# Hybrid encoder trunk: band added on VectorE, rotary product from PSUM, first convolution steps on ScalarE, more weight buffers

## The chip, the cores and the metric

The kernel runs on one core of a Trainium2 chip, as one program. The metric is the time of one execution in device microseconds. In the profile the engines are PE (TensorE, matrix products), PEld (its weight loads), DVE (VectorE), ACT (ScalarE), POOL (GpSimd) and SP (SyncE, whose queue issues most DMAs).

## The reference, cut to what matters

The reference is a two-layer bidirectional encoder on two inputs with shared weights: a prompt of 1024 tokens and a sample of 512, both 1024 wide, in float32.

```python
def even_layer(...):                       # layer 0
    u = h @ w_in
    glu, a_gate, q, k, v, b_gate = split_cols(u, EVEN_SPLITS)
    a = a_val * jax.nn.sigmoid(a_glu)
    a = layernorm(depthwise_conv(a, conv_w, conv_b), ln_g, ln_b)      # 31 taps
    a = jax.nn.silu(a) * jax.nn.silu(a_gate)
    q = apply_rope(q, cos, sin); k = apply_rope(k, cos, sin)
    o = windowed_gqa(q, k, v, sink) * jax.nn.silu(b_gate)             # keys within 128 tokens
    return jnp.concatenate([a, o], axis=-1) @ w_out

def windowed_gqa(q, k, v, sink):
    scores = jnp.where(mask, q . k * dh ** -0.5, -jnp.inf)
    probs = softmax(concatenate([scores, sink_logit]))[..., :-1]
    return probs . v

def odd_layer(...):                        # layer 1
    # differential attention: softmax(q1.k1) - lam * softmax(q2.k2), per-head norm, gate
    # Mamba-2 scans forward and backward, behind a 5-tap depthwise convolution
    return jnp.concatenate([c, d], axis=-1) @ w_out
```

Rotary embedding is `x * cos + rotate_half(x) * sin`. An RMS norm stands ahead of each layer and at the end, and each layer adds its input.

## The kernel before

**Tiles.** Activations lie with channels on the 128 partitions and tokens along the free dimension, in three chunks `g` of 512 tokens (two of the prompt, one of the sample). A projection (`proj`, L273 to L283) makes a 128x512 block: over eight slices of the input it adds three float32r products, L280 (high weight by high input), L281 (high by low) and L282 (low by high), so 24 matmuls into one PSUM bank.

**Weights.** `load_w` (L258) brings a tile of weights in two halves of 128x512. For each half SP issues the load into `wr` (L267), ACT writes the rounded high part `wh` (L268) and POOL subtracts it to make the low part `wl` (L269). Each of the three has three buffers for the whole kernel, so one and a half tiles. A half serves all three chunks.

**Stages.** `phase` opens pools for each stage from the table `PHASES`: A1 (gated convolution, rotary q and k, v), A2 (sliding attention, output projection of layer 0), B1a (short convolution), B1z (z and v of layer 1), B1b (scans, rotary of layer 1), B2 (differential attention), O1 (the last output projections). `SHARED` lists tiles with buffers for all stages, among them `e2`, the 128x512 scratch of the evacuations (four). Projections have one PSUM bank `pj` and, in some stages, further `pjx`: four in A1, one in A2, none in B1b.

**Order.** The code puts units of work beside one another (`merge`, `spread`). A planner then orders the instructions of each engine with a timeline of its own, by when operands and buffers come free there, and the order is fixed in the program. On the chip each engine takes its instructions in that order and waits on semaphores. So another buffer count or another instruction can change the order of much else.

**Convolution (A1).** For each of four blocks of channels `glu_units` makes the gated input `a`, and `conv_units` (L435) filters it on DVE: odd taps, even taps and their sums accumulate in three tiles `fir`. `begin` starts them with L444, L446 and L447 (multiply by the first tap, two of them with a bias), then `taps` runs L453, L456 and L458, each of which reads two tiles of SBUF. `conv_ln` (L475) normalizes all four.

**Rotary.** `rope` (L375) is called 15 times in A1 and 24 times in B1b. ACT copies the product from PSUM to `r` (L378), four DMAs exchange the half heads into `rs` (L381), DVE multiplies `r` by the cosine in place (L382), POOL multiplies `rs` by the sine (L383), DVE adds (L384) and SP stores (L385). `r` and `rs` are `e2` tiles.

**Sliding attention (A2).** For each block `b` of 128 queries and each key head `g`, `scores` handles four query heads:

```python
T_.matmul(o, qh, kk, start=True, stop=False)                 # L553
T_.matmul(o, ql, kk, start=False, stop=False)                # L554
T_.matmul(o, ident_r, cr[...], start=False, stop=True)       # L555, adds 0 or -1e30
V.tensor_reduce(out=mx, in_=o, op=ALU.max, negate=True)      # L558
V.tensor_tensor(out=mx, in0=mx, in1=nsink, op=ALU.min)       # L559
S.activation(out=pr, in_=o, func=AF.Exp, bias=mx, accum_out=den)   # L561
```

There are 12 blocks, so 96 such tiles: 64 of 384 keys and 32 of 256. The scores have three PSUM banks, `s1`. The probabilities `pr` (eleven tiles) are scaled on POOL (L569), transposed on PE (L584), split into high and low parts (L201 on ACT, L202 on DVE, to `pT`) and multiplied by the values (L587, L588); L589 and L590 put out the result. `values` runs one group behind `scores`. Gate projections (`gate2`: ACT L371, DVE L372) and the output projection run beside it.

**Others that the change touches.** `xbc` (L705) is the short convolution: L713 starts it on DVE, L716 runs the other four taps, L718 applies the activation. `diff_units` in B2 has, for each block of queries, L979 (square of a denominator times a constant), L981, L982 (the ratio) and L984 (difference of the two maps).

## Time and profile before

| quantity | value |
|---|---|
| median of 3 runs | 1711.17 us (1710.85 to 1715.9) |
| profiled execution, its own time | 1710.5 us |
| its span, first to last instruction | 1708.7 us |
| mean granted TensorE clock | 0.979 |
| instructions | 22696 |
| HBM traffic over the span | 127 GB/s |

The profiled execution is one of its own, 0.7 us below the median; about 1.8 us of its time lie outside the span. A line of the waits names who waited, for what, the sum in us, how often and the longest. A line of a group gives source line, engine, operation, tiles and shapes, the count, then busy time, mean duration in ns, and the idle time of the engine ahead of it with what ended it. `pjx<-x,wl` means that a tile `pjx` is written from `x` and `wl`. A matmul's duration runs from its start to its modelled end, and matmuls overlap.

### The profile page before, as it was taken

Reading aid. Unit: us, or ns where it says so; the run is one execution under the profiler, and the core shown is the slowest. Engines: PE = TensorE matmul, PEld = TensorE weight load, DVE = VectorE, ACT = ScalarE, POOL = GpSimd, SP = SyncE. Lnnn points to the kernel's source line nnn. Section 1 sums busy time; section 2 is a strip of 40 time slices with the busy share of each in tenths; the row PEclk is TensorE's granted clock in tenths of the full one; section 3 lists DMA queues with packets and bytes.
Section 4 is the critical chain, followed back from the end, with each engine's and each line's share of the span. In section 5 each row is a group of like instructions: output and inputs, shape, how many; then the busy total and the mean of one; then the engine's idle time right before and its main releaser. Section 6 shows DMA issues by size and latency. Waiting matters only on the chain.

```text
span 1708.7 us, 22696 instructions
## 1 busy us (share of the span) xinstructions
PE 1586.7 (93%) x7868; PEld 1303.6 (76%) x7868; DVE 1132.5 (66%) x1631; ACT 708.1 (41%) x1440; POOL 677.5 (40%) x531
## 2 busy tenths in 40 slices
PE   4998998889988989999999999989998999999997
PEld 3776787668777867867788887778877877888887
DVE  6788999954788786646664003796635677678554
ACT  6210111144676664433433112222225767668542
POOL 4244333333656545631311004654444534442340
PEclk9999999989999999999999999999999999999999
DMA  9011023335455447731433216664553545442562
GB/s 371 29 53 47 32 74 98 113 104 175 126 169 184 150 145 232 236 111 37 131 105 130 78 50 189 198 180 141 158 150 124 149 131 147 138 133 75 178 198 99
DMA packets 159109, 229.45 MB, mean 134 GB/s; under 512 B 18279, under 2 KB 70567, under 8 KB 158994
## 3 DMA queue, kind: packets, MB, share of 16 engines
q1 hardware_dynamic: 157074, 227.40, 42.2%
q8 instruction: 62, 1.02, 0.3%
q0 software_dynamic: 1920, 0.59, 0.2%
q14 instruction: 53, 0.43, 0.1%
HBM read 153.15 MB, written 64.55 MB: 127 GB/s over the span
## 4 chain that ended last, share of the span: by engine, by line
PE 30%; DMA 7%; DVE 4%; issue 4%; POOL 2%; SPq 2%; ACT 2%; POOLq 0%; DVEq 0%; ACTq 0%
PE ms L992 3%; PE pj L280 3%; PE pj L281 3%; PE pj L282 3%; DMA e<-e 2%; PE pjx L747 2%; PE pjx L746 2%; PE pjx L748 2%; PE s L967 2%; PE s L968 2%; PE pjx L280 1%; PE pjx L281 1%; PE pjx L282 1%; POOL e L383 1%; PE tr L390 1%
## 5 line engine op out<-in xcount | busy, mean ns | idle before, releaser
L269 POOL TENSOR_TENSOR wl<-wr,wh 128x512 fp32r<-128x512 f32 (+1 forms) x169 | 274.0, 1625 | 366.0 <-ACT wh L268 325.7
L282 PE MATMUL pjx<-x,wl 128*128 128x512 f32 (+1 forms) x712 | 286.4, 404 | 19.9 <-POOL wl L269 19.9
L280 PE MATMUL pjx<-x,wh 128*128 128x512 f32 (+1 forms) x712 | 287.4, 404 | 12.5 <-DVE e L372 8.0
L281 PE MATMUL pjx<-x,wh 128*128 128x512 f32 (+1 forms) x712 | 287.9, 405 | 6.3 <-DVE x L202 5.0
L280 PE MATMUL pj<-x,wh 128*128 128x512 f32 x604 | 247.4, 410 | 9.3 <-DVE e L372 5.0
L281 PE MATMUL pj<-x,wh 128*128 128x512 f32 x604 | 244.3, 404 | 3.9 <-DVE x L202 3.9
L282 PE MATMUL pj<-x,wl 128*128 128x512 f32 x604 | 241.9, 400 | 0.0
L268 ACT ACTIVATE wh<-wr 128x512 fp32r<-128x512 f32 (+1 forms) x169 | 105.5, 625 | 205.9 <-PE pjx L281 86.5
L282 PEld LDWEIGHTS pjx<-x,wl 128*128 128x128 f32 (+1 forms) x712 | 135.2, 190 | 55.5 <-POOL wl L269 23.0
L280 PEld LDWEIGHTS pjx<-x,wh 128*128 128x128 f32 (+1 forms) x712 | 134.8, 189 | 49.6 <-DVE e L372 10.4
L281 PEld LDWEIGHTS pjx<-x,wh 128*128 128x128 f32 (+1 forms) x712 | 134.8, 189 | 41.4 <-DVE x L202 6.6
L280 PEld LDWEIGHTS pj<-x,wh 128*128 128x128 f32 x604 | 115.6, 191 | 36.0 <-DVE e L372 6.1
L281 PEld LDWEIGHTS pj<-x,wh 128*128 128x128 f32 x604 | 115.3, 191 | 30.2 <-DVE x L202 5.1
L282 PEld LDWEIGHTS pj<-x,wl 128*128 128x128 f32 x604 | 115.3, 191 | 26.5 <-issue 0.2
L383 POOL TENSOR_TENSOR e<-e,cs 128x512 f32<-128x512 f32 x39 | 64.8, 1660 | 106.5 <-DMA e<-e 96.9
L976 ACT ACTIVATE pr<-s,nmx 128x1024 f32<-128x1024 f32 (+1 forms) x96 | 93.3, 975 | 27.6 <-DVE nmx L970 15.7
L177 POOL TENSOR_TENSOR r<-v,mhalf 128x4 f32<-128x4 f32 (+2 forms) x37 | 33.0, 892 | 140.5 <-DVE v L173 91.6
L992 PE MATMUL ms<-v,pT 128*128 128x128 f32 x640 | 81.2, 278 | 6.5 <-ACT pT L989 4.0
L992 PEld LDWEIGHTS ms<-v,pT 128*128 128x128 f32 x640 | 77.9, 193 | 10.6 <-ACT pT L989 4.4
L970 DVE TENSOR_REDUCE nmx<-s 128x1 f32<-128x1024 f32 x64 | 76.8, 1217 | 10.1 <-PE s L968 9.7
L517 POOL TENSOR_TENSOR raw<-raw,q 128x1024 fp32r<-128x1024 f32 x24 | 58.2, 2425 | 53.4 <-ACT q L515 49.0
L569 POOL TENSOR_SCALAR pr<-pr,den 128x384 f32<-128x384 f32 (+1 forms) x96 | 55.4, 597 | 50.0 <-DVE den L567 26.2
(360 smaller groups left out, 3393.1 us busy)
## 6 DMA issues: line engine op xcount, KB each, us to landing
wr<-in_wo SPq DMA_DIRECT2D x96, 256.0 KB, 3.7
wr<-in_w SPq DMA_DIRECT2D x87, 256.0 KB, 3.0
e<-e SPq DMA_DIRECT2D x156, 64.0 KB, 2.0
x<-xbd SPq DMA_DIRECT2D x22, 384.0 KB, 3.9
ct<-x1d SPq DMA_DIRECT2D x29, 256.0 KB, 3.6
raw<-q0d SPq DMA_DIRECT2D x48, 128.0 KB, 3.0
ct<-cat0d SPq DMA_DIRECT2D x24, 256.0 KB, 3.1
x1d<-e SPq DMA_DIRECT2D x24, 256.0 KB, 3.1
```

The lines of the kernel that those rows point to most:

```text
L268: S.activation(out=wh, in_=raw, func=AF.Copy)
L269: G.tensor_tensor(out=wl, in0=raw, in1=wh.bitcast(F32), op=ALU.subtract)
L280: T_.matmul(acc, wh[:, kk, :], xh[:, k, :], start=(k == ks[0]), stop=False)
L281: T_.matmul(acc, wh[:, kk, :], xl[:, k, :], start=False, stop=False)
L282: T_.matmul(acc, wl[:, kk, :], xh[:, k, :], start=False, stop=(k == ks[-1]))
L383: G.tensor_tensor(out=rs, in0=rs, in1=cs_["sin"][:, cs], op=ALU.mult)
L517: G.tensor_tensor(out=lo, in0=raw, in1=q.bitcast(F32), op=ALU.subtract)
L569: G.tensor_scalar(out=prs[j], in0=prs[j], scalar1=den[:, j:j + 1], scalar2=1.0, op0=ALU.mult, op1=ALU.mult)
L746: T_.matmul(acc, xh[:, k, ts], hi[k], start=(k == 0), stop=False)
L970: V.tensor_reduce(out=nmx[:, t:t + 1], in_=o, axis=AX.XY, op=ALU.max, negate=True)
L976: S.activation(out=pr, in_=o if ncs > 1 else o[:, u:u + 1, :], func=AF.Exp, bias=nmx[:, u:u + 1], accum_out=den[:, u:u + 1])
L992: T_.matmul(oacc, pT[:, i, :], vtok[:, kt, :], start=(kt == 0), stop=(kt == NB - 1))
```

## The change

Six things are done.

The sliding scores lose the mask matmul. One DVE instruction reads the scores from PSUM and the band (`ngt`, 0 or -1e30, now a constant in SBUF), writes the negated sums to `pr` and keeps their minimum, begun at the negated sink. ACT's exponential then reads `pr` instead of PSUM, with a scale of -1. `pr` has ten tiles instead of eleven; `cr` loses its middle block.

`rope` multiplies by the cosine straight from PSUM into a third `e2` tile.

The first steps of both convolutions become activations on ACT (L444, L446, L447 and L713 go from DVE).

`wr`, `wh` and `wl` get two further buffers each in A1, one in B1b and three in O1; `e2` gets two in A1 and one in B1b.

The differential attention computes the square times a constant once for four blocks instead of for each, and keeps the ratio in a tile of its own.

A tile `pad` of 32 bytes is allocated among the small tiles.

```diff
-    "A1": (dict(cs=2, a=2, xs=1, fir=3, y6=5), ...
+    "A1": (dict(e2x=2, wrx=2, whx=2, wlx=2, cs=2, a=2, xs=1, fir=3, y6=5), ...
-    "A2": (dict(... pr=11, q6=2), ...
+    "A2": (dict(... pr=10, q6=2), ...
-    "B1b": (dict(rk=2, ...
+    "B1b": (dict(e2x=1, wrx=1, whx=1, wlx=1, rk=2, ...
-    "O1": (dict(sq=4, ct=16, ss=1, fin=8), dict(pjx=5)),
+    "O1": (dict(wrx=3, whx=3, wlx=3, sq=4, ct=16, ss=1, fin=8), dict(pjx=5)),
-SHARED = dict(wr=3, e2=4, bcs=1)
+SHARED = dict(wr=3, wh=3, wl=3, e2=4, bcs=1)
...
     def sb(tag, shape, dt=F32):
+        extra = ph["sb"].get(tag + "x", 0)
+        if extra:
+            n = ph["sb", tag] = (ph.get(("sb", tag), -1) + 1) % (SHARED[tag] + extra)
+            if n >= SHARED[tag]:
+                tag += "x"
...
+    V.memset(tiny(8, "pad", 1), 0.0)
...
-    cr = const([P, 4, P], "cr", dt=F32R)
-    ngt = sb("fir", (P, 3, P))
+    cr = const([P, 3, P], "cr", dt=F32R)
+    ngt = const([P, 3, P], "ngt")
...
+    band = ngt.rearrange("p b c -> p (b c)")
...
     def rope(acc, scale, g, dst):
-        r, rs = sb("e2", (P, CH)), sb("e2", (P, CH))
+        r, rs, o = (sb("e2", (P, CH)) for _ in range(3))
         S.activation(out=r, in_=acc, func=AF.Copy, scale=scale)
+        V.scalar_tensor_tensor(out=o, in0=acc, scalar=scale, in1=cs_["cos"][:, cs], op0=ALU.mult, op1=ALU.mult)
...
-        V.tensor_tensor(out=r, in0=r, in1=cs_["cos"][:, cs], op=ALU.mult)
         G.tensor_tensor(out=rs, in0=rs, in1=cs_["sin"][:, cs], op=ALU.mult)
-        V.tensor_tensor(out=r, in0=r, in1=rs, op=ALU.add)
-        dma(out=dst[:, tok(g)], in_=r)
+        V.tensor_tensor(out=o, in0=o, in1=rs, op=ALU.add)
+        dma(out=dst[:, tok(g)], in_=o)
...
-            V.tensor_scalar(out=f[0], in0=a[:, :, 1:512:2], scalar1=cwh[:, j, 0:1], ...
-            V.tensor_scalar(out=f[1], in0=a[:, :, 0:513:2], scalar1=cwh[:, j, 1:2], scalar2=None, op0=ALU.mult)
-            V.tensor_scalar(out=f[2], in0=xs[:, :, 0:256], scalar1=cws[:, j, 0:1], ...
+            S.activation(out=f[0], in_=a[:, :, 1:512:2], func=AF.Identity, scale=cwh[:, j, 0:1], bias=...)
+            S.activation(out=f[1], in_=a[:, :, 0:513:2], func=AF.Copy, scale=cwh[:, j, 1:2])
+            S.activation(out=f[2], in_=xs[:, :, 0:256], func=AF.Identity, scale=cws[:, j, 0:1], bias=cb2[:, j:j + 1])
...
-                T_.matmul(o, ql[:, g, j, :], kk[g][:, k0 * P:k1 * P], start=False, stop=False)
-                T_.matmul(o.rearrange("p (b c) -> p b c", c=P), ident_r, cr[...], start=False, stop=True)
+                T_.matmul(o, ql[:, g, j, :], kk[g][:, k0 * P:k1 * P], start=False, stop=True)
-                V.tensor_reduce(out=mx, in_=o, axis=AX.X, op=ALU.max, negate=True)
-                V.tensor_tensor(out=mx, in0=mx, in1=nsink[:, 4 * g + j:4 * g + j + 1], op=ALU.min)
-                S.activation(out=pr, in_=o, func=AF.Exp, bias=mx, accum_out=den[:, j:j + 1])
+                V.tensor_tensor_reduce(out=pr, in0=o, in1=band[...], scale=-1.0, scalar=nsink[:, 4 * g + j:4 * g + j + 1],
+                                       op0=ALU.add, op1=ALU.min, accum_out=mx)
+                S.activation(out=pr, in_=pr, func=AF.Exp, bias=mx, scale=-1.0, accum_out=den[:, j:j + 1])
...
-        V.tensor_scalar(out=acc, in0=a[:, :, 0:CH], scalar1=prm[:, wc:wc + 1], ...
+        S.activation(out=acc, in_=a[:, :, 0:CH], func=AF.Identity, scale=prm[:, wc:wc + 1], bias=...)
...
-            V.tensor_scalar(out=st_["e"][:, b % 4:b % 4 + 1], in0=den[:, 0:1], scalar1=den[:, 0:1], scalar2=EPS, ...
...
             if c == 3:
+                e = st_["e"][:, 0:4]
+                V.scalar_tensor_tensor(out=e, in0=e, scalar=EPS, in1=e, op0=ALU.mult, op1=ALU.mult)
```

## Prediction

> **What bounds the kernel now.** I read the page's shares first, then the windows by stage, then what PE waits for, then single lines.

> ```profile
> PE 1586.7 (93%) x7868; PEld 1303.6 (76%) x7868; DVE 1132.5 (66%) x1631; ACT 708.1 (41%) x1440; POOL 677.5 (40%) x531
> ```

> PE leads at 93%, but the share is an average. The windows (length; busy PE, PEld, DVE, ACT, POOL; granted clock; DMA) part it, in order: convolution with its projections; layer norm and gates; sliding attention; a projection stretch; the scans; differential attention.

> ```profile
> 62.00:342.00 280.00, 257.01 (x1075) 204.33 (x1074) 257.38 (x272) 38.60 (x67) 104.01 (x47) 0.97 0.22 66
> 342.00:400.00 58.00, 51.66 (x234) 40.76 (x233) 29.51 (x51) 27.53 (x43) 17.83 (x12) 0.91 0.38 131
> 400.00:655.00 255.00, 233.05 (x1176) 191.71 (x1175) 192.05 (x418) 159.65 (x390) 139.47 (x150) 0.98 0.52 158
> 655.00:1030.00 375.00, 370.09 (x1676) 295.29 (x1675) 176.67 (x207) 119.19 (x188) 103.32 (x73) 1.00 0.38 121
> 1030.00:1283.00 253.00, 238.65 (x1160) 196.76 (x1159) 160.37 (x195) 66.41 (x105) 130.29 (x126) 0.99 0.57 171
> 1283.00:1600.00 317.00, 302.12 (x1789) 259.51 (x1788) 226.61 (x337) 224.19 (x514) 125.00 (x79) 0.98 0.40 121
> ```

> The projection stretch is PE's alone (370 of 375). In the convolution stage DVE is as full as PE, 257 each of 280: there two engines bind in turn. In the sliding attention PE has 233 of 255, DVE 192. So work taken off PE counts nearly in full where PE is full, and work taken off DVE counts where PE waits for it:

> ```profile
> PE pjx L282 <- POOL wl L269: 19.9, 7, 6.4
> PE s L553 <- ACT pr L561: 9.9, 13, 2.1
> PE pjx L280 <- DVE e L372: 8.0, 3, 4.2
> PE trx L584 <- DVE pT L202: 5.6, 4, 2.4
> PE ms L588 <- DVE pT L202: 2.7, 2, 2.5
> ```

> The first is a wait for low weight parts, the second for a score bank, the rest are DVE late with PSUM or with probabilities.

> **Fused scores: the mask product goes.** Each of 96 score tiles loses its third matmul (L555).

> ```profile
> L555 PE MATMUL s<-cr x96: 277/336/522, 375.3 to 624.2; 128*128 128x384 f32 x64, 128*128 128x256 f32 x32
> ```
> ```profile
> 439.98 0.40 PE L280 MATMUL pj<-x,wh 128*128 128x512 f32 x1
> ...
> 441.38 0.40 PE L280 MATMUL pj<-x,wh 128*128 128x512 f32 x1
> ...
> 442.73 0.34 PE L554 MATMUL s<-k,raw 128*128 128x384 f32 x1
> 442.91 0.34 PE L555 MATMUL s<-cr 128*128 128x384 f32 x1
> 443.09 0.40 PE L588 MATMUL ms<-pT,v 128*128 128x512 f32 x1
> ```

> A matmul's duration is its latency. What it takes from PE is the distance of starts: 0.233 us for 512 columns (six starts in 1.40 us, at full clock), by columns 0.175 for 384 (0.18 in the rows) and 0.117 for 256: 64 x 0.175 + 32 x 0.117 = **14.9 us**, on PE's path.

> **Fused scores: DVE.** A reduction and a tiny minimum become one pass that adds the band, writes the negated scores and keeps their minimum.

> ```profile
> L558 DVE TENSOR_REDUCE nmx<-s 128x1 f32<-128x384 f32 (+1 forms) x93 | 46.0, 507 | 7.1 <-PE s L555 6.5
> L559 DVE TENSOR_TENSOR nmx<-nmx,nsink 128x1 f32<-128x1 f32 x93 | 38.6, 426 | 0.4
> ```

> This is the attention's window: 84.6 us for the pair, the minimum at 426 ns although one element wide. The new pass reads as many columns as the reduction and one SBUF operand beside PSUM. No such instruction is in the trace: below, the reduction alone, 0.507 us; above, the pair, 0.933, or the reduction with a second cycle per element, about 0.95. I take 0.6, nearest to the reduction, so DVE sheds about 93 x 0.33 = 31 of its 192 us. The bank is free after DVE instead of after the exponential, which reads SBUF now. Against the waits: 9.9 for banks and 5.6 + 2.7 for probabilities, 18.2 in all, and the 2% of 255 us = 5 us that the clock lacked. I credit **13 us**, as chains over three engines stay. The probability tiles fall from 11 to 10 and DVE claims them earlier, with all its queue behind; ten still hold two groups of four with two over, so I price this at nothing, 2 us if the planner packs it tighter.

> **Weight buffers in the convolution stage.** Three half-tile sets become five. Why the low part is late:

> ```profile
> L269 POOL TENSOR_TENSOR wl<-wr,wh x31: 1264/1737/12249, 62.4 to 332.3; 128x512 fp32r<-128x512 f32 x31
>   PE pjx L282: 15.9, 4
> ```
> ```profile
> 143.59 1.01 DVE L453 SCALAR_TENSOR_TENSOR fir<-a,cwh,fir 128x768 f32<-128x768 f32 x1
> 144.52 1.01 DVE L456 SCALAR_TENSOR_TENSOR fir<-a,cwh,fir 128x771 f32<-128x771 f32 x1
> ```

> One subtraction on POOL takes 1.26 us or up to 12.25, the long ones while DVE runs filter steps back to back. [...] PE then waits for the low part, 15.9 us in four gaps. A half weight feeds 36 matmuls of 0.233 us = 8.4 us, so two more halves put 17 us of PE's work between a stalled subtraction and PE: the gaps close. The loads move ahead on SP's queue, past the rotary shuffles; with a DMA share of 0.22 I price that at nothing. Each of the longer ones also leaves the clock low:

> ```profile
> 96.32 0.79 PE L282 MATMUL pjx<-x,wl 128*128 128x512 f32 x1 [4.00 <-POOL wl L269]
> ...
> 97.34 0.63 PE L281 MATMUL pjx<-x,wh 128*128 128x512 f32 x1
> 97.77 0.63 PE L282 MATMUL pjx<-x,wl 128*128 128x512 f32 x1
> 98.19 0.63 PE L280 MATMUL pjx<-x,wh 128*128 128x512 f32 x1
> ```
> ```profile
> 85.40:213.60 128.20, 114.39 (x469) 90.96 (x468) 113.43 (x127) 17.56 (x30) 54.24 (x17) 0.93 0.15 44
> ```

> Behind the gap starts are 0.425 us apart, and over 128 us the clock lacks 7%: 9 us. Together 25. [...]

> **Convolution and rotary on DVE.** If PE no longer stalls, DVE must keep up, so its relief decides how much of the 25 is kept.

> ```profile
> L444 DVE TENSOR_SCALAR fir<-a,cwh,prm 128x768 f32<-128x768 f32 x4 | 4.3, 1064 | 0.0
> L447 DVE TENSOR_SCALAR fir<-xs,cws,cb 128x768 f32<-128x768 f32 x4 | 4.2, 1059 | 0.0
> L446 DVE TENSOR_SCALAR fir<-a,cwh 128x771 f32<-128x771 f32 x4 | 4.0, 1004 | 0.0
> L718 ACT ACTIVATE y<-y 128x1536 f32<-128x1536 f32 x8 | 11.9, 1488 | 21.3 <-DVE y L716 21.3
> ```
> ```profile
> L382 DVE TENSOR_TENSOR e<-e,cs 128x512 f32<-128x512 f32 x39 | 42.2, 1081 | 41.3 <-DMA e<-e 38.7 <-DMA bc<-bcd 1.7 <-DMA pvd<-nx 0.8
> L372 DVE SCALAR_TENSOR_TENSOR e<-e,pj 128x512 f32<-128x512 f32 x22 | 15.0, 683 | 18.4 <-ACT e L371 18.3
> ```

> First steps: 12.5 us leave DVE; on ACT 768 columns cost between half of 1.488 and DVE's 1.06 us, so 9 to 13 us on an engine with 241 us free. Behind three such steps, 3 us, an evacuation of PSUM may wait on ACT; five banks take projections here, so PE goes on, and without them it would be 4 x 3 = 12 us. Rotary: the cosine product ran 39 times at 1.081 us with two SBUF inputs; with one in PSUM the like row is 0.683, a saving of 0.4 each: 6 us over the stage's 15 calls, 10 over the scans' 24. It also no longer waits for the shuffle's DMA (38.7 us of DVE idleness). Together 18.5 of DVE's 257 us here. DVE would then need 239 us against the 255 I forecast. I credit **22 us** to 62:400: 20 of the 25, and 2 of the 8.0 for L372, whose banks come free sooner when DVE is less full.

> **The rest.** The eight first steps of the short convolution leave DVE in the projection stretch, where PE covers them: nothing, and at most a microsecond either way if ACT is late with an evacuation. In the scans rotary needs three of five e2 buffers instead of two of four, and the one pj bank is held until DVE, too, has read it: between 8 lost and 10 won, nothing taken. Differential attention drops a tiny DVE step from a chain:

> ```profile
> DVE e L979 <- ACT pr L976: 12.9, 16, 1.7
> ```

> The reciprocal inherits that wait and only the step's length goes, behind PE's other work: 1 us. Three more sets of weights at the end: 1 us, bounds 0 to 3, as PE seldom waits there. The pad shifts what is allocated after it by 32 bytes; no row shows an address to matter: nothing, see the second rival.

> **Sum.** 14.9 + 13 + 22 + 1 + 1 = 52 us off the profiled execution's 1710.5 (span 1708.7 and 1.8 around), 0.7 under the median: 1658.5, so **1659 us** on the median. A difference of 0.3%, 5 us, is about what a measurement of this kernel can tell. Every line's order is planned anew, which moves waits elsewhere by some microseconds; with 0.507 and 0.95 us for the fused pass, and 12 to 25 for the weights, this case alone spans 1641 to 1677.

> **Rivals.**
> *DVE stays the bound.* The fused pass costs 0.95 us, as the pair did, and the filter steps keep DVE full. Then only a third of the mask's 15 shows, the bank and probability waits stay, and the convolution stage keeps 15 of its 25: 20 us, 1690. For it: DVE equals PE at 257 us. Against: the reduction reads the same columns at 0.507. [...]

> *The address matters.* By the sizes of the tiles ahead of them, the x16 buffers and most stage buffers begin 32 bytes past a multiple of 64 and would now begin on one. Starts of 512 columns at half clock are 0.425 us apart, so the stream alone at full clock is 0.2125; they are 0.233, in L282 here and in L280 and L281 alike:

> ```profile
> L282 PE MATMUL pjx<-x,wl 128*128 128x512 f32 (+1 forms) x712 | 286.4, 404 | 19.9 <-POOL wl L269 19.9
> L282 PE MATMUL pj<-x,wl 128*128 128x512 f32 x604 | 241.9, 400 | 0.0
> ```

> 1316 matmuls on each of three lines, 0.0205 us each above the stream: at most 81 us. A third of it gives 27 more: 1632. Against: nothing says that the address is the cause.

> *Rotary holds the bank.* In the scans each of 24 projections goes through one bank. If the planner puts the new product behind a long DVE instruction, PE stands:

> ```profile
> L865 DVE TENSOR_TENSOR p<-p,p x12: 1209/1222/2648, 1049.9 to 1257.1; 128x1024 f32<-128x1024 f32 x12
> ```

> With 2.65 us and its own 0.68 that is 3.3 us, 24 times, 80 us: 1739, slower. It decides from 57/24 = 2.4 us per call. Against: DVE is busy 160 of 253 us there, and PE has scan products to run meanwhile.

> **How the numbers follow.** Forecast 0.52, address 0.20, DVE bound 0.19, bank 0.09. Faster: 0.52 + 0.20 + 0.16 + 0 = 0.88; same 0.03 + 0.02 = 0.05; slower 0.07. From 1618 to 1698 leaves out the bank case and the far end of the address case, under 2 in 10.

> **What would show it.** L555 gone, and the pass's row near 0.6 us (at 0.95, DVE stays the bound). Subtractions in the convolution stage may still take 10 us, but PE no longer waits for L269 there, and the clock from 85 to 213 is above 0.98. The cosine product at 0.68 us. Starts of 512-column matmuls still 0.233 apart (0.225 or less would be the address). PE idle before L280 behind the cosine product in the scans would prove the bank. I am wrong if 62:400 and the attention together shrink by less than 35 us.

## The result and the profile after

| quantity | before | after |
|---|---|---|
| median, lowest to highest of 4 runs each | 1711.0 us (1708.45 to 1715.9) | 1660.5 us (1654.65 to 1667.45) |
| ratio, 95% interval | 1 | 0.9703 (0.966 to 0.9747) |
| profiled execution, its own time | 1710.5 us | 1667.45 us |
| its span | 1708.7 us | 1665.7 us |
| matmuls | 7868 | 7772 |

The median fell by 50.5 us; the prediction had 52. The profiled execution of the changed kernel is the longest of its four, 7 us over their median, so the traces alone account for 43 us. The granted clock was 0.977 in it and 0.981 to 0.984 in the other three. Lines moved: 269 became 276, 280 to 282 became 287 to 289, 372 is 380, 382 is L387, 384 is L392, 453, 456 and 458 are L460, L463 and L465, 558 is L564.

The page's first part, after:

```profile
PE 1560.7 (94%) x7772; PEld 1293.3 (78%) x7772; DVE 1076.2 (65%) x1576; ACT 733.6 (44%) x1461; POOL 663.8 (40%) x531
```

The next two fences are windows cut at the same three marks in each kernel: last convolution tap, last matmul of the sliding attention's values, last z and v product; the rest is not shown. Columns: window, length, busy PE, PEld, DVE, ACT, POOL, granted clock, DMA share, GB/s. Before:

```profile
62.00:337.70 275.70, 253.66 (x1062) 201.93 (x1061) 253.15 (x268) 38.60 (x67) 104.01 (x47) 0.97 0.21 64
337.70:650.70 313.00, 283.76 (x1403) 231.43 (x1402) 224.02 (x459) 185.68 (x430) 155.42 (x161) 0.97 0.49 153
650.70:1030.50 379.80, 374.89 (x1696) 299.14 (x1696) 178.44 (x221) 120.69 (x191) 105.21 (x74) 1.00 0.39 123
```

After:

```profile
62.00:315.80 253.80, 237.99 (x1037) 195.40 (x1036) 247.66 (x258) 50.88 (x80) 98.13 (x45) 0.98 0.21 65
315.80:609.00 293.20, 275.86 (x1333) 223.42 (x1332) 204.21 (x460) 187.72 (x430) 158.61 (x161) 0.96 0.53 164
609.00:987.00 378.00, 371.40 (x1690) 299.05 (x1689) 161.00 (x204) 134.22 (x200) 97.73 (x68) 0.99 0.38 122
```

The convolution window is 21.9 us shorter, the attention window 19.8, the projection stretch 1.8. The marks part the work of DVE and of the attention alike, but not all of PE's: 25 matmuls fewer lie in the first window, and in the second 70 fewer, where the mask alone is 96, so some 6 us of projections moved from the first into the second. The sum of the two, 42 us, is not touched by that. From 1030.5 to the end it was 678.2 us, from 987.0 it is 678.7: no gain between these two executions, of which the second is a long one (the next section compares this stretch over all kernels). So all that this trace shows lies in the two stages where the prediction put 50 of its 52 us, and it is 42 there.

The new pass and its readout, and what PE waits for, after:

```profile
L564 DVE CUSTOM_DVE_ANT_0 pr<-s,ngt,nsink x96: 455/608/619, 380.3 to 586.1; 128x384 f32<-128x384 f32 x64, 128x256 f32<-128x256 f32 x32
L564 DVE DVE_READ_ACCUMULATOR2_ANT nmx<- x96: 77/83/88, 380.7 to 586.5; 128x1 f32 x96
```
```profile
PE pj L287 <- DVE e L380: 13.2, 5, 7.4
...
PE s L972 <- ACT pr L981: 7.5, 8, 2.6
PE s L560 <- DVE nmx L564: 6.8, 7, 2.7
PE pj L289 <- POOL wlx L276: 5.6, 1, 5.6
```

The pass's median is 0.608 us, and a second instruction of 0.083 us reads the minimum out. The wait for low weight parts, 19.9 us before on this list, is down to 5.6 in one place and 1.9 in two others; the first place went to the gates (L380), where DVE is late with a bank of PSUM. The gates' wait itself has not changed: 8.0 and 5.0 us in two lines before, 13.2 now.

The subtraction on POOL in the convolution stage, and the clock's window there, after:

```profile
L276 POOL TENSOR_TENSOR wlx<-wrx,whx x10: 1292/1997/17272, 90.4 to 265.7; 128x512 fp32r<-128x512 f32 x10
```
```profile
85.40:213.60 128.20, 122.60 (x541) 101.02 (x540) 128.20 (x137) 25.47 (x39) 51.90 (x19) 0.99 0.18 53
```

One subtraction is still starved, 17.3 us now, and yet PE waits for it 5.6 us only; the clock went from 0.93 to 0.99. In this window DVE is busy for 128.20 of 128.20 us: it has become the bound.

### The profile page after: what moved, and what is told of

Read it like the earlier page. It is cut to its first block, busy times and chain, and to the rows that moved or that the text cites. A ratio compares the mean times of both kernels' runs of the same rounds, so it can differ in the third digit from the quotient of the medians.

```text
span 1665.7 us, 22451 instructions
## 1 busy us (share of the span) xinstructions
PE 1560.7 (94%) x7772; PEld 1293.3 (78%) x7772; DVE 1076.2 (65%) x1576; ACT 733.6 (44%) x1461; POOL 663.8 (40%) x531
## 4 chain that ended last, share of the span: by engine, by line
PE 32%; DMA 6%; issue 4%; DVE 4%; POOL 2%; ACT 2%; SPq 1%; POOLq 0%; DVEq 0%; ACTq 0%
PE pj L287 3%; PE pj L288 3%; PE pj L289 3%; PE ms L994 2%; PE pjx L752 2%; PE pjx L751 2%; PE pjx L753 2%; PE pjx L288 1%; PE pjx L289 1%; PE s L972 1%; PE pjx L287 1%; PE s L973 1%; DMA ct<-g2d 1%; PE tr L398 1%; DMA raw<-k1d 1%
## 5 line engine op out<-in xcount | busy, mean ns | idle before, releaser
L276 POOL TENSOR_TENSOR wl<-wr,wh 128x512 fp32r<-128x512 f32 (+1 forms) x147 | 208.5, 1423 | 281.0 <-ACT wh L275 275.7
L287 PE MATMUL pj<-x,wh 128*128 128x512 f32 x536 | 219.6, 410 | 19.2 <-DVE e L380 13.2
L288 PE MATMUL pjx<-x,wh 128*128 128x512 f32 (+1 forms) x576 | 229.1, 398 | 4.4 <-DVE x L209 4.4
L287 PE MATMUL pjx<-x,wh 128*128 128x512 f32 (+1 forms) x576 | 228.8, 398 | 2.9 <-ACT wh L275 2.7
L289 PE MATMUL pjx<-x,wl 128*128 128x512 f32 (+1 forms) x576 | 228.1, 397 | 1.9 <-POOL wl L276 1.9
L288 PE MATMUL pj<-x,wh 128*128 128x512 f32 x536 | 215.7, 402 | 4.0 <-DVE x L209 3.9
L289 PE MATMUL pj<-x,wl 128*128 128x512 f32 x536 | 216.1, 403 | 0.0
L275 ACT ACTIVATE wh<-wr 128x512 fp32r<-128x512 f32 (+1 forms) x147 | 91.4, 623 | 138.7 <-PE pj L288 50.2
L287 PEld LDWEIGHTS pj<-x,wh 128*128 128x128 f32 x536 | 103.9, 194 | 44.4 <-DVE e L380 15.5
L288 PEld LDWEIGHTS pjx<-x,wh 128*128 128x128 f32 (+1 forms) x576 | 107.9, 187 | 29.6 <-DVE x L209 5.6
L287 PEld LDWEIGHTS pjx<-x,wh 128*128 128x128 f32 (+1 forms) x576 | 107.9, 187 | 27.5 <-ACT wh L275 3.1
L289 PEld LDWEIGHTS pjx<-x,wl 128*128 128x128 f32 (+1 forms) x576 | 107.9, 187 | 27.1 <-POOL wl L276 3.2
L288 PEld LDWEIGHTS pj<-x,wh 128*128 128x128 f32 x536 | 103.9, 194 | 26.3 <-DVE x L209 5.6
L524 POOL TENSOR_TENSOR raw<-raw,q 128x1024 fp32r<-128x1024 f32 x24 | 58.8, 2451 | 45.5 <-ACT q L522 33.0
L972 PE MATMUL s<-k,q 128*128 128x512 f32 x160 | 68.4, 428 | 7.7 <-ACT pr L981 7.5
```

The source lines that it names most:

```text
L275: S.activation(out=wh, in_=raw, func=AF.Copy)
L276: G.tensor_tensor(out=wl, in0=raw, in1=wh.bitcast(F32), op=ALU.subtract)
L287: T_.matmul(acc, wh[:, kk, :], xh[:, k, :], start=(k == ks[0]), stop=False)
L288: T_.matmul(acc, wh[:, kk, :], xl[:, k, :], start=False, stop=False)
L289: T_.matmul(acc, wl[:, kk, :], xh[:, k, :], start=False, stop=(k == ks[-1]))
L524: G.tensor_tensor(out=lo, in0=raw, in1=q.bitcast(F32), op=ALU.subtract)
```

## The experiments

Marks of each kernel's profiled execution (us from its start), and the median of its runs with the ratio to the kernel before:

| kernel | last tap | last values | last z, v | median | ratio, 95% interval |
|---|---|---|---|---|---|
| before | 337.7 | 650.7 | 1030.5 | 1711.0 | |
| before_pad | 338.2 | 651.7 | 1030.3 | 1706.4 | 0.9959 (0.9941 to 0.9978) |
| before_scores | 336.8 | 629.4 | 1011.0 | 1697.3 | 0.9895 (0.9867 to 0.9924) |
| before_scores_weights_pad | 334.4 | 629.2 | 1007.0 | 1689.2 | 0.9860 (0.9830 to 0.9890) |
| three_parts | 317.8 | 609.2 | 987.1 | 1670.1 | 0.9754 (0.9733 to 0.9776) |
| after_old_scores | 315.1 | 628.6 | 1004.3 | 1687.6 | 0.9856 (0.9825 to 0.9886) |
| after_old_conv | 330.0 | 625.7 | 1001.8 | 1675.4 | 0.9777 (0.9748 to 0.9806) |
| after_old_weights | 322.7 | 618.3 | 996.1 | 1679.4 | 0.9799 (0.9773 to 0.9826) |
| after_no_pad | 316.3 | 611.7 | 991.0 | 1664.4 | 0.9714 (0.9690 to 0.9739) |
| after_old_rope | 317.7 | 610.6 | 988.9 | 1660.3 | 0.9687 (0.9657 to 0.9717) |
| after | 315.8 | 609.0 | 987.0 | 1660.5 | 0.9703 (0.9660 to 0.9747) |
| after_add_pool | 321.4 | 622.2 | 999.6 | 1672.2 | 0.9771 (0.9751 to 0.9790) |
| after_low_act | 294.6 | 591.2 | 966.8 | 1637.3 | 0.9570 (0.9549 to 0.9591) |

The distance of a kernel from the changed one is good to about 9 us, both intervals taken together; the first three marks resolve more, since they are near the cause, but each is one execution. The stretch from the last z and v product to the end varies most: in after, after_no_pad and after_pad_consts, whose instructions stand in the same order, it takes 678.7, 669.1 and 675.5 us. Over all kernels it is 667 to 682 us (mean 674) in the nine that have five `e2` buffers in the scans and the shorter chain in the differential attention, and 678 to 686 (mean 682) in the five that have neither. So the changed kernel's later stages probably gain some 8 us that its own profiled execution does not show; that is argued from single executions. The theory at the start was the prediction's: buffers take PE's stalls away, and DVE's relief decides how much of that is kept. Rivals: the buffers alone hold the gain; the pad does.

**The scores.** Once taken out of the changed kernel, once put alone into the kernel before (the same edit, reversed). Both kernels have ten probability tiles, so the step from eleven to ten was not tried by itself.

```diff
-    T_.matmul(o, qh, kk, ...); T_.matmul(o, ql, kk, ..., stop=True)
-    V.tensor_tensor_reduce(out=pr, in0=o, in1=band, ..., accum_out=mx)
-    S.activation(out=pr, in_=pr, func=AF.Exp, bias=mx, scale=-1.0, ...)
+    T_.matmul(o, qh, ...); T_.matmul(o, ql, ...); T_.matmul(o, ident_r, cr[...], stop=True)
+    V.tensor_reduce(out=mx, in_=o, op=ALU.max, negate=True)
+    V.tensor_tensor(out=mx, in0=mx, in1=nsink, op=ALU.min)
+    S.activation(out=pr, in_=o, func=AF.Exp, bias=mx, ...)
```

> The changed kernel with the old scores (mask matmul, reduction, minimum). The record's theory: 15 + 13 = 28 us more, 1688. Rival, the fused pass is worth the mask product alone: 15 more, 1675, with the waits for the score bank the same with or without it.

> The kernel before with the fused scores alone (no mask matmul, ten probability tiles). The forecast for this part was 14.9 + 13 = 28 us, the run without it gave 27: 1682 to 1686 us, ratio 0.983 to 0.986, all of it between the first and the last score, the convolution stage as before (taps end at 338 us). The rival, that the scores gain only together with the buffers, because a stage behind a stalled one waits for the same weights: 1690 us or more.

Measured: 27 us longer without them, by the medians, and 18 shorter, by the ratio, with them alone: 1697.3 us, outside the 1682 to 1686 expected and in the rival's range. The marks agree better. From the last tap to the last values the kernel takes 313.0 us with the old scores (before) or 313.5 (after_old_scores), and 293.2 (after) or 292.6 (before_scores) with the new ones: 20 to 21 us either way. That window of before_scores:

```profile
336.80:629.40 292.60, 269.21 (x1296) 215.81 (x1295) 203.94 (x458) 187.95 (x428) 154.92 (x160) 0.96 0.53 162
```

Against before, PE's busy time falls by 283.76 - 269.21 = 14.6 us with 107 matmuls fewer, the 96 mask products (forecast 14.9) and 11 others. Its idle time falls from 313.00 - 283.76 = 29.2 to 23.4 us, so the waits gave 6 us where 13 were forecast. From after_old_scores to the changed kernel the busy time falls by 12.4 us with 90 matmuls fewer, and the idle time by 8.0. With the other matmuls counted at 0.23 us each, the 96 took 12 to 14 us of PE. So the rival's reason, that the scores gain only together with the buffers, does not hold: the window is as much shorter without them. What before_scores lacks in its median is lost behind 1011 us, where it takes 686.1 us and the kernel before 678.2. The other way round, the two profiled executions of after_old_scores and the changed kernel differ by 20.3 us; the 27 of the medians hold the 7 us by which the latter lies over its median.

**The weight buffers.** Taken out of the changed kernel in all stages, and, only in the convolution stage, put into the kernel before beside scores and pad.

```diff
-    "A1": (dict(e2x=2, wrx=2, whx=2, wlx=2, cs=2, ...
+    "A1": (dict(e2x=2, cs=2, ...
-    "B1b": (dict(e2x=1, wrx=1, whx=1, wlx=1, rk=2, ...
+    "B1b": (dict(e2x=1, rk=2, ...
-    "O1": (dict(wrx=3, whx=3, wlx=3, sq=4, ...
+    "O1": (dict(sq=4, ...
```

> The changed kernel with three weight buffers in every stage (e2 keeps its extra ones). The record's theory: PE again waits some 16 us for low weight parts in the convolution stage and the clock falls there, 20 us more, 1680. Rival, with DVE relieved the old buffers would do: under 5 us more, 1660 to 1665.

> The kernel before with three parts alone: the fused scores (ten probability tiles), two further buffers each of wr, wh and wl in the convolution stage only, and the 32-byte pad. Rotary, convolutions, e2 buffers, the differential attention and the buffers of the later stages are as before. The sum of the parts measured so far is 27 + 19 + 4 = 50, as much as the whole change: if the rest is worth nothing, 1660 to 1663 us, ratio 0.970 to 0.972. The theory of the prediction, that DVE's relief of 18.5 us decides how much of the weights' 25 is kept: 1668 to 1675 us, ratio 0.975 to 0.979.

Measured: 19 us more without them in the one by the medians, though its marks and its span are only 7 to 9 us later, the changed kernel's execution being a long one. In the other only 8 us less than with scores alone, pad included, and outside both ranges expected (1660 to 1663 and 1668 to 1675); the last tap comes at 334.4 instead of 336.8 us. The sum of parts taken out one by one (27 + 19 + 4 = 50) would have given 1661 there; it was 1689.2. So the parts are not additive, and something that is not in this kernel carries much of the gain. What DVE waited for up to the last tap, in the kernel before, then in before_scores_weights_pad, then in after_old_weights:

```profile
DVE a L430 <- PE pjx L282: 12.2, 4, 5.9
DVE a L430 <- PE pj L282: 6.2, 1, 6.2
```
```profile
DVE a L438 <- PE pj L289: 5.8, 1, 5.8
DVE a L438 <- PE pjx L289: 0.8, 1, 0.8
```
```profile
DVE a L438 <- PE pjx L289: 10.8, 2, 5.4
DVE a L438 <- PE pj L289: 5.8, 1, 5.8
```

DVE makes the gated input (L430, later L438) as soon as PE has its projection. A subtraction starved on POOL stalls PE, and PE's stall reaches DVE: 18.4 us of DVE's time before. The buffers take 12 of these 18 away. But DVE's own work then fills the window, as before_scores_weights_pad shows:

```profile
62.00:334.40 272.40, 249.36 (x1082) 204.59 (x1080) 259.60 (x271) 42.17 (x73) 119.26 (x47) 0.96 0.22 67
```

DVE is busy for 259.6 of 272.4 us, 6 more than the 253.15 before, so of the 12 us only 2 to 3 come out. PE's gap has not closed either. What PE waits for there up to the last tap, and the subtraction behind it:

```profile
PE pj L289 <- POOL wlx L276: 13.2, 1, 13.2
```
```profile
L276 POOL TENSOR_TENSOR wlx<-wrx,whx x10: 1272/2002/24922, 90.1 to 271.9; 128x512 fp32r<-128x512 f32 x10
```

One subtraction lasts 24.9 us, longer than the 17 us of matmuls that two more halves hold, and PE waits 13.2 us for it, where with the scores alone (before_scores) it waited 19.8 us in six gaps of the whole execution. The ten subtractions into `wlx` take 45.5 us together here; in after_old_conv, below, they take 42.9 and PE waits 12.1. With the first steps on ACT the two are 36.9 and 5.6 us (changed kernel, its longest subtraction 17.3) and 40.0 and 6.9 (three_parts). So with DVE's relief POOL's subtractions were shorter too; by what mechanism, no run shows.

**The first steps of the convolutions.** Put back on DVE in the changed kernel.

```diff
-    S.activation(out=f[0], in_=a[:, :, 1:512:2], func=AF.Identity, scale=cwh[:, j, 0:1], bias=...)
+    V.tensor_scalar(out=f[0], in0=a[:, :, 1:512:2], scalar1=cwh[:, j, 0:1], scalar2=..., op0=ALU.mult, op1=ALU.add)
...
-    S.activation(out=acc, in_=a[:, :, 0:CH], func=AF.Identity, ...)
+    V.tensor_scalar(out=acc, in0=a[:, :, 0:CH], ..., op0=ALU.mult, op1=ALU.add)
```

> The changed kernel with the first steps of both convolutions on DVE again, as before. The theory of the prediction: 12.5 us come back to DVE in the convolution stage, where it is full for at least half of the time, the steps of the short convolution are covered by PE; so 5 to 12 us longer, 1666 to 1672 us, and the convolution taps end 5 to 12 us later than at 316 us. The rival, that the buffers alone hold the gain: 1660 us, within 3, with the taps ending later but the layer norm's wait taken up by other projections.

Measured: 15 us longer (12.7, give or take 9, by the ratios), 3 more than the 5 to 12 expected; the last tap 14.2 us later, more than the 12.5 us of work that came back. This is the part that was missing above: the four parts taken out one by one now make 27 + 19 + 4 + 15 = 65 us, of 50. With it and without buffers (after_old_weights) the last tap is at 322.7, with buffers and without it at 330.0, with both at 315.8.

**Scores, buffers in the convolution stage, first steps and pad, nothing else.** The kernel before_scores_weights_pad with the edit above reversed.

```diff
-    V.tensor_scalar(out=f[0], ...); V.tensor_scalar(out=f[1], ...); V.tensor_scalar(out=f[2], ...)
+    S.activation(out=f[0], ...); S.activation(out=f[1], ...); S.activation(out=f[2], ...)
...
-    V.tensor_scalar(out=acc, in0=a[:, :, 0:CH], ...)
+    S.activation(out=acc, in_=a[:, :, 0:CH], func=AF.Identity, ...)
```

> The kernel before with the fused scores, two further buffers each of wr, wh and wl in the convolution stage, the first steps of both convolutions on ACT, and the pad. Rotary, e2, the differential attention and the buffers of the later stages as before. If the gain lies in DVE's first steps together with the buffers, and the parts left out are worth nothing: 1658 to 1664 us, ratio 0.969 to 0.973, taps end at 316 to 319 us. The rival, that the rotary change or the e2 buffers carry part of the gain beside the others: 1668 us or more.

Measured: last tap, last values and last z product as in the changed kernel within 2 us, so these parts carry all of the gain up to 987 us. The median is still 9.5 us above, in the rival's range; by the ratios that is 0.0051, give or take 0.0048, hardly resolved. The scans differ most: from the last z product to the last product of the scans (L880 in the changed kernel) this kernel takes 239 us, the kernel before 232, the changed one 225.5, and the kernels with five `e2` buffers there and any other edit 224 to 230. But to the end the two profiled executions differ by 2 us only (680.8 against 678.7), so where the 9.5 us of the medians arise is not shown, and which part left out here brings them was not tried by itself.

**The rotary product.** The old one in the changed kernel, its buffers kept.

```diff
-        r, rs, o = (sb("e2", (P, CH)) for _ in range(3))
+        r, rs = sb("e2", (P, CH)), sb("e2", (P, CH))
...
-        V.scalar_tensor_tensor(out=o, in0=acc, scalar=scale, in1=cs_["cos"][:, cs], op0=ALU.mult, op1=ALU.mult)
...
+        V.tensor_tensor(out=r, in0=r, in1=cs_["cos"][:, cs], op=ALU.mult)
...
```

> The changed kernel with the rotary product of before: ACT copies from PSUM, DVE multiplies the copy in place by the cosine after the shuffle was issued. The theory of the prediction: the cosine product goes back from 0.69 to about 1.08 us, 15 times in the convolution stage and 24 times in the scans; in the convolution stage DVE is full (100% busy from 85 to 213 us), so its 6 us come back there, in the scans nothing: 1664 to 1668 us, ratio to before 0.972 to 0.975. The rival, that with five weight buffers PE has cover enough and DVE's relief counts for nothing: 1660 us, within 3. The rival of the held bank: PE gains in the scans without the second reader of pj: 1655 or less.

Measured: 1660.3 us, the same; last tap 2 us later. The theory's 4 to 8 us are not there. The reason shows in DVE's two rotary lines up to the last tap: the cosine product and the addition before, then after (by buffer; of the product's four groups there the largest is shown).

```profile
L382 DVE TENSOR_TENSOR e<-e,cs 128x512 f32<-128x512 f32 x15 | 16.3, 1089 | 0.4 <-DMA e<-e 0.3
L384 DVE TENSOR_TENSOR e<-e,e 128x512 f32<-128x512 f32 x15 | 12.4, 823 | 0.0
```
```profile
L387 DVE SCALAR_TENSOR_TENSOR e<-pjx,cs 128x512 f32<-128x512 f32 x7 | 4.8, 680 | 0.0
...
L392 DVE TENSOR_TENSOR e2x<-e2x,e2x 128x512 f32<-128x512 f32 x7 | 10.2, 1460 | 0.0
L392 DVE TENSOR_TENSOR e<-e,e 128x512 f32<-128x512 f32 x8 | 6.5, 816 | 0.0
```

The product fell to 0.68 us as forecast, 15 times 10.3 us in all; but the addition, which reads two SBUF tiles, grew from 12.4 to 16.7. Together 28.7 became 27.0. In after_old_rope itself the old product takes 13.4 us there, not 16.3, and the addition 14.6: 28.0 us, one more than in the changed kernel.

**Who lengthens DVE's steps.** The filter steps have a median of 1.01 us in the changed kernel, and 176 of them take 205.4 us, not 178. Two kernels ask whether POOL does it: one leaves the subtraction out and lets ACT copy the raw weights in its place, one gives POOL the rotary addition.

```diff
-            G.tensor_tensor(out=wl, in0=raw, in1=wh.bitcast(F32), op=ALU.subtract)
+            S.activation(out=wl, in_=raw, func=AF.Copy)        # convolution stage alone
```

> The changed kernel, but in the convolution stage ACT writes the low weight parts as a copy of the raw weights instead of POOL's subtraction; the subtraction is left out there, and the output is not the reference's. It takes 30 subtractions (69 us) off POOL and gives ACT 30 copies of 0.63 us. Theory, that POOL and DVE slow each other: the filter steps, which have a median of 1.01 us but take 205 us for 176 (177 without interference), fall to 190 or less, the subtractions' 17 us starvation is gone, and the taps end 8 to 20 us earlier than at 316: 1642 to 1652 us. The rival, that the filter steps are long for a reason of their own: 203 to 207 us for the 176, taps end within 3 us of 316, 1657 to 1664 us.

```diff
-        V.tensor_tensor(out=o, in0=o, in1=rs, op=ALU.add)
+        G.tensor_tensor(out=o, in0=o, in1=rs, op=ALU.add)      # convolution stage alone
```

> The changed kernel with the rotary addition of the convolution stage on POOL instead of DVE: 15 additions, 16.7 us, leave DVE, which is full there. If DVE's own work sets the end of the taps: 8 to 16 us earlier than at 316, 1646 to 1654 us. The rival, that POOL's two-input steps cost DVE as much as they take from it: taps end within 3 us of 316 or later, 1658 to 1668 us, with the filter steps' 205 us grown by about as much as the additions had taken.

The filter steps up to the last tap, in the changed kernel, in after_low_act (three lines further down) and in after_add_pool:

```profile
L460 DVE SCALAR_TENSOR_TENSOR fir<-a,cwh,fir 128x768 f32<-128x768 f32 x60 | 71.1, 1184 | 0.1
L465 DVE SCALAR_TENSOR_TENSOR fir<-xs,cws,fir 128x768 f32<-128x768 f32 x60 | 70.9, 1182 | 0.0
L463 DVE SCALAR_TENSOR_TENSOR fir<-a,cwh,fir 128x771 f32<-128x771 f32 x56 | 63.4, 1132 | 0.0
```
```profile
L468 DVE SCALAR_TENSOR_TENSOR fir<-xs,cws,fir 128x768 f32<-128x768 f32 x60 | 66.6, 1110 | 0.0
L466 DVE SCALAR_TENSOR_TENSOR fir<-a,cwh,fir 128x771 f32<-128x771 f32 x56 | 63.6, 1136 | 0.0
L463 DVE SCALAR_TENSOR_TENSOR fir<-a,cwh,fir 128x768 f32<-128x768 f32 x60 | 62.7, 1046 | 0.1
```
```profile
L460 DVE SCALAR_TENSOR_TENSOR fir<-a,cwh,fir 128x768 f32<-128x768 f32 x60 | 82.1, 1368 | 0.2
L465 DVE SCALAR_TENSOR_TENSOR fir<-xs,cws,fir 128x768 f32<-128x768 f32 x60 | 79.0, 1317 | 0.0
L463 DVE SCALAR_TENSOR_TENSOR fir<-a,cwh,fir 128x771 f32<-128x771 f32 x56 | 68.2, 1218 | 0.0
```

205.4 us in the changed kernel, 192.9 without the subtractions, 229.3 with the additions on POOL. The first is less of a fall than the 190 expected, but DVE is busy for 24 us less in all there, the last tap comes 21 us earlier and the time falls by 23 us, the last two more than expected. Not all of that need come from POOL and DVE slowing each other, as PE has no low parts to wait for any more. PE is then the bound, busy for all 232.60 us of the window at full clock:

```profile
62.00:294.60 232.60, 232.60 (x1034) 192.57 (x1033) 223.24 (x256) 63.96 (x105) 30.12 (x18) 1.00 0.23 71
```

In the second, DVE gave away 16.7 us of additions and its filter steps grew by 23.9: 12 us slower, the rival's outcome, 4 us beyond its range. So the two runs show that POOL's work beside the filter steps costs DVE too: with less of it the 176 steps take 192.9 us, with more 229.3, against 205.4. By what mechanism, no run shows.

**The pad.** Taken out of the changed kernel, put alone into the kernel before, and moved in the changed kernel. None of the three edits changes the instructions of the other lines or their order; the buffers' addresses alone differ.

```diff
-    V.memset(tiny(8, "pad", 1), 0.0)                 # after_no_pad; added in before_pad
+    V.memset(const([P, 8], "pad"), 0.0)              # after_pad_consts
```

> The changed kernel without the 32-byte tile; the order of instructions on every engine is the changed kernel's. The record's theory (the pad is worth nothing): 1660 us, and starts of the projections' 512-column matmuls stay 0.227 us apart. The address theory (the pad is what moved them from 0.234 to 0.227): 0.234 again, 3984 x 7 ns = 28 us more PE work, 15 to 25 us of it in the time, 1675 to 1686.

> The kernel before with the 32-byte tile alone, same order of instructions. The record's theory: 1711 us, starts 0.234 us apart. The address theory: 0.227, and 15 to 25 us less, 1686 to 1696; less than that where PE waits for another engine anyway.

> The changed kernel with the 32 bytes of padding among the constants instead of the small tiles; the instructions and their order are the same. The weights wr, wh and wl then begin 32 bytes past a multiple of 64, the inputs x16 on a multiple. If the start of the moving operand decides, starts of 512-column projections stay 0.227 us apart; if it is that weights and moving operand begin in the same class, they go back to 0.233, as in the kernel before, where the weights begin on a multiple of 64 and the inputs 32 past one.

Measured: 4 us longer without it, which the intervals do not resolve, and 5 shorter with it alone (7 by the ratio, 0.9959), which they do. The marks of before_pad do not show the gain: its profiled execution is the longest of its twelve, 6.5 us over their median, at a granted clock of 0.970. Starts of the changed kernel's 512-column projections, first and last of 24 in a row:

```profile
129.75 0.39 PE L287 MATMUL pjx<-x,wh 128*128 128x512 f32 x1
...
134.96 0.39 PE L289 MATMUL pjx<-x,wl 128*128 128x512 f32 x1
```

5.21 us over 23 distances are 0.227 us, where the kernel before had 0.233. With the padding among the constants (1663.4 us in its one run) both occur within one projection:

```profile
129.72 0.40 PE L287 MATMUL pjx<-x,wh 128*128 128x512 f32 x1
...
135.09 0.40 PE L289 MATMUL pjx<-x,wl 128*128 128x512 f32 x1
135.32 0.39 PE L287 MATMUL pjx<-x,whx 128*128 128x512 f32 x1
...
137.82 0.40 PE L289 MATMUL pjx<-x,wlx 128*128 128x512 f32 x1
```

24 matmuls with weights in `wh` and `wl` are 5.37 / 23 = 0.233 us apart, the next 12, with weights in the stage's own buffers `whx` and `wlx`, 2.50 / 11 = 0.227, with the same input. By the sizes of the tiles ahead of them the inputs begin on a multiple of 64 bytes here, `whx` and `wlx` too, `wh` and `wl` 32 past one. In the kernel before it was the inputs that began 32 past and the weights that did not: 0.233; in the changed kernel neither does: 0.227. The z products of the kernel before, where both operands began 32 past, were 0.227 apart already:

```profile
919.68 0.39 PE L748 MATMUL pjx<-zw,x 128*128 128x512 f32 x1
...
923.08 0.39 PE L748 MATMUL pjx<-zw,x 128*128 128x512 f32 x1
```

3.40 us over 15 distances. Without the pad, after_no_pad has both cases with inputs 32 past: 0.233 with `wh` and `wl` on a multiple, 0.227 with `whx` and `wlx` 32 past, in the median of the projections' distances; in before_pad that median is 0.227 throughout. So neither operand's own start decides, but whether the two agree modulo 64 bytes. Why, no run shows.

## Why the prediction was right, point by point

**Right in sum, 50.5 us against 52.** Of it the trace shows 42 us in the two stages where 50 were put; the remaining 8 lie between the profiled execution and the median of its kernel, and no trace of that kernel places them. Other kernels' traces put about as much into the later stages, for which the prediction had 2. That the sum came within 2 us is in part luck: the attention's waits gave less than was credited, and the pad and probably the later stages gave what was priced at nothing or almost nothing.

**Mask product**, 14.9 us: 12 to 14 us of PE's busy time in the two pairs of kernels. Right.

**The fused pass**, 0.6 us, between 0.507 and 0.95: 0.608 and 0.083 for the readout. The upper bound was the author's estimate; by the reduction's own rows, 0.548 us for 384 columns and 0.416 for 256, a column took 1.03 ns, and that twice would make 0.94 for 384, where the pass took 0.613. Pass and readout make 60 us for 96 tiles of both widths, where the pair took 84.6 for 93. DVE sheds 27 us by these lines, 31 were forecast; the window's busy time falls by 18 to 20. The second instruction was not foreseen.

**"I credit 13 us"** for the attention's waits: mis-sized, 6 to 8 us. Bank waits did not vanish but changed hands, 6.8 us behind the pass (9.9 before, behind the exponential), and the window's clock went from 0.97 to 0.96, so the 5 us that the clock lacked were not won.

**"I credit 22 us" in the convolution stage:** 21.9, but the step "20 of the 25, and 2 of the 8.0" split it wrongly. It gave the buffers the gain and the first steps the keeping of it. At the last tap the buffers bring 2 us beside the scores and the pad (336.8 to 334.4); all other parts without the buffers, of which the first steps are the largest, bring 14 (336.8 to 322.7); everything together, 21. No kernel has the first steps alone, but three_parts, which lacks the rotary product and the further `e2` buffers, is only 2 us later than the changed kernel at that mark. DVE was the closer bound: its 253 busy and 18.4 us of waits for PE filled 271.6 of 275.7 us. The prediction saw DVE as full as PE, but did not look up what DVE itself waited for. That wait was PE's stall, and the buffers' gain could come out only as fast as DVE's own work left room.

That step also took the long subtractions as POOL's loss alone, while DVE's filter steps fell from 205.4 to 192.9 us where these were left out (after_low_act), and set 17 us of cover against subtractions of 12.25 us at most, where one took 24.9 with the buffers and 17.3 after. "The gaps close" held in the changed kernel but for one wait of 5.6 us, and not in the two kernels with buffers and the first steps on DVE, where 12 to 13 us stayed; the clock's 0.99 is above the 0.98 named. Of the 25 us the clock's 9 were too many: before, the clock stood at 0.5 for 17.1 us of that window, and PE was busy in 13.4 of them, so 6.7 us of work were lost, and the rest of the 9 fell into the gaps that were counted already. The 2 of the 8.0 us for L372 did not come: the gates' wait is 13.2 us after, as the two lines of before together.

**Rotary:** the forecast 0.68 us was met, the saving of 6 us in the convolution stage was not, as the addition grew. In the scans the forecast was nothing, between 8 lost and 10 won. Nothing shows the held bank: PE waits for L387 for 2.9 and 2.7 us in the whole execution. A part of the 9.5 us by which three_parts lags may be the scans' extra buffers, which is argued and not tried.

**The pad, "no row shows an address to matter: nothing":** the failed step. It is worth about 5 us (0.9959, 0.9941 to 0.9978). The rival had the work right and the time wrong: its stream of 0.2125 us, half of the 0.425 at a granted clock of 0.50, was an estimate, and the distance went from 0.233 to 0.227; a third of its 20.5 ns came true, 6 ns on each of 3948 matmuls, 24 us of PE's work, yet 5 us of time. That PE is the bound alone in few stages can be only a part of the reason. In the projection stretch, where it is, 958 such matmuls should have given 5.7 us; the window shrank by 1.8 in the changed kernel and by 1.2 with the pad alone. The granted clock there fell from 1.00 to 0.99 in both, and over whole executions from 0.974 in the mean of the kernel before to 0.972 with the pad alone. Where the rest of the 24 us went stays open.

**DVE stays the bound:** half true, and not for the price of the pass. In the changed convolution stage DVE is full again, 247.7 of 253.8 us, and the gain came in spite of it, because DVE has less to do there.

The bound that the prediction set itself, that the two stages shrink by 35 us at least, was met with 42. The last buffers and the shorter chain in the differential attention, 1 us each, were not tried alone.

## What to carry to other kernels

Where two engines of a stage are both over nine tenths busy, as PE and DVE were here with 253.7 and 253.2 of 275.7 us, look up what each waits for: when each waits for the other, single parts measured one by one neither add up nor tell their worth, and the relief of the one decides what the other's buffers bring. Before work goes from DVE to POOL, count what it costs DVE's other steps: the rotary additions handed to POOL freed 16.7 us of DVE and lengthened its filter steps by 23.9, while first steps handed to ACT brought the end of the stage forward by 14 us. An operand in PSUM shortened its own step from 1.09 to 0.68 us, but the time did not follow (1660.3 us without it, 1660.5 with it). And count the distance of matmul starts before and after a change of allocation: 32 bytes shifted it from 0.233 to 0.227 us here.
